# A two-layer hybrid encoder on one core: attention divides its output instead of its probabilities, and VectorE makes all low parts of the mixer's weights

## The chip, the core and the metric

The kernel runs on one core of one Trainium2 chip. The metric is the device time of one launch in microseconds (us). The core has a TensorE for matmuls (PE in the rows; PEld is its weight load), VectorE (DVE), ScalarE (ACT) and GpSimd (POOL) for everything elementwise, and SyncE (SP), which here only issues transfers from device memory. Each engine runs its own queue of instructions in order and waits on semaphores for the others.

## The reference, cut to what matters

Two layers over 512 tokens of width 1024, all in float32. Each layer runs an attention group and a state-space (SSD) group side by side on one normalised input, joins them through one output projection, and then runs a SwiGLU FFN.

```python
def reference(x, ...):
    for i in range(DEPTH):                       # DEPTH = 2
        h = rms_norm(x, norm_mix_w[i])
        proj = jnp.einsum("bld,de->ble", h, w_in[i])
        q, k, v, z, xbc_raw, dt_raw = jnp.split(proj, split_at, axis=-1)
        q = rms_norm(q.reshape(b, l, N_Q_HEADS, HEAD_DIM), q_norm_w[i])    # 8 heads of 64
        k = rms_norm(k.reshape(b, l, N_KV_HEADS, HEAD_DIM), k_norm_w[i])   # 2 heads of 64
        q = axial_rope(q, cos_r, sin_r, cos_c, sin_c)
        k = axial_rope(k, cos_r, sin_r, cos_c, sin_c)
        attn_out = blocked_gqa(q, k, v)
        ssd_out = ssd_mixer(z, xbc_raw, dt_raw, ...)   # conv, chunked scans both ways, gate, norm
        mixed = jnp.concatenate([attn_out, ssd_out], axis=-1)
        x = x + jnp.einsum("ble,ed->bld", mixed, w_out[i])
        h = rms_norm(x, norm_ffn_w[i])
        x = x + swiglu(h, w_gate[i], w_up[i], w_down[i])
    return rms_norm(x, final_norm_w)

def one_block(qi):                               # 128 queries against all 512 keys
    s = jnp.einsum("bqgrd,bkgd->bgrqk", qi, k)
    p = jax.nn.softmax(s, axis=-1)
    return jnp.einsum("bgrqk,bkgd->bqgrd", p, v)
```

## The kernel before

**Products in three parts.** To keep float32 accuracy at the faster matmul type, every weight chunk and every activation is split into a high part (a rounded copy) and a low part (the value minus that copy), and each product is three matmuls: high by high, high by low, low by high. `Stream.split` (lines 180 to 195) makes the parts of a weight chunk of 128x1024: for each 512 columns ScalarE casts `whi` (line 192) and VectorE or GpSimd subtracts to get `wlo` (line 193). Which of the two engines does it is chosen per chunk: the names in `POOL_LO` (line 56) and the four chunks of the SSD half of `w_out` (line 122) go to GpSimd, which makes 16 chunks per layer, 32 in all, in 64 instructions. Chunks are split two ahead of their use.

**The mixer of a layer** (`mixer`, lines 446 to 939) first projects k, v and dt, and then runs three generators by turns (line 930). `fill` goes through `ORDER`: the eight x/B/C chunks with their convolution (`xbc`), the two halves of q (`qproj`) and of z; then, once the SSD half is done, the SSD half of the output projection, `out_half(1, ...)`, 8 output tiles of 12 matmuls; then it waits for attention and splits attention's output into `mixed.h` and `mixed.l` (lines 851 to 855). `ssd` runs the scans and the gated norm and writes its part of `mixed` through `to_mixed`. `att` walks the 8 pairs of a key head g and a block c of 128 queries, four query heads (tiles) each, so 32 tiles per layer. After the three, `out_half(0, ...)` adds the attention half.

**A tile of attention** (lines 663 to 695): two matmuls give the scores in PSUM (668, 669); VectorE takes the negative row maximum (671) and multiplies it by `qri`, the reciprocal norm of the query (672); ScalarE takes the exponential with `qri` as scale and the row sum beside it (674); VectorE takes the sum's reciprocal (675) and multiplies the 128x512 probabilities by it (679); TensorE transposes them in four pieces (682); ScalarE copies them to SBUF (92); TensorE multiplies by the values (692); ScalarE copies the result back into `qr` (92). `queries` prepares the four heads: a ScalarE copy `qd`, four transposes (656), a cast `qh` and a difference `ql` (659, 660).

**Order.** Nothing here is ordered by hand inside an engine. The kernel is traced in the order of the generators, that order gives each instruction its priority, and a planner with a time model of its own lays out each engine's queue when the program is built: the most urgent instruction whose inputs and buffers its model calls ready goes next. On the chip each queue then runs in that fixed order. Helper lines hide several operations: line 92 holds ScalarE copies, line 95 the `tensor_tensor` of VectorE or GpSimd; there one goes by tile names.

The probabilities live in a ring of four 128x512 slots (`ring("p")`), their transposes in another.

Of the kernel before, what the change touches and what calls it, by code (L numbers as in the profile page):

```python
# [15 lines left out]
F32 = mybir.dt.float32  # L16
F32R = mybir.dt.float32r
I32 = mybir.dt.int32
AF = mybir.ActivationFunctionType
# [17 lines left out]
NPAIR = (NF - PLAIN) // 2  # L37
SRAW = 6

NORM = "VVVV"  # L40
PTE = "AAAA"
GGE = "GG"
QDE, OUTE, _, YE, HE, WE, RAE, MLE, DSE = "AAVGVGVVG"
EB, GGB = 2, 4
DDW, DDE = 512, "A"
MORE = "VGGVG"
# [6 lines left out]
YS = 1  # L53
NA, NF_, NS = 1, 2, 3
ORDER = "x4 q0 x5 x7 x6 x3 x0 x1 x2 q1 z0 z1".split()
POOL_LO = "x3 x5 x7 z0 z1 x4 x6 q1 x1".split()
EPS = 1e-6
KVDT = 272

# [11 lines left out]
def merge(a, b, c):  # L71
    return a.rearrange("p (b c) -> p b c", b=b, c=c)


def bc(ap, shape, axis):
    return ap.unsqueeze(axis).broadcast_to(shape)
# [3 lines left out]
def tile_hybrid_encoder(ctx, tc, xt_d, par_d, rope_d, snw_d, w_kvdt, w_xbc, w_q, w_z, w_out, w_gate, w_up, w_down, out_d):  # L80
# [10 lines left out]
    def copy(e, out, in_):  # L91
        A.copy(out, in_) if e == "A" else (G if e == "G" else V).tensor_copy(out, in_)

    def tt(e, *args):
        (G if e == "G" else V).tensor_tensor(*args)
# [9 lines left out]
    def stream(src, n, lo=0, cut=WU):  # L105


        chunks.append((src, n, lo, cut))

    for l in range(L):  # L110
        for i in range(2):
            for j in range(2):
                stream(w_kvdt[l, i, :, 2 * j * KVDT:2 * (j + 1) * KVDT], 2 * KVDT)
        for what in ORDER:
            i, lo = int(what[1]), what in POOL_LO
            if what[0] == "x":
                stream(w_xbc[l, i], 1024, lo, 512)
            else:
                for j in range(2):
                    stream({"q": w_q, "z": w_z}[what[0]][l, 2 * i + j], 1024, lo, 512)  # L120
        for i in range(4):
            stream(w_out[l, 1, i], 1024, 1, 512)
        for i in (2, 3, 0, 1):
            stream(w_out[l, 0, i], 1024, 0, 512)
        for f in range(PLAIN):
            stream(w_gate[l, f], 1024)
            stream(w_up[l, f], 1024)
        for a, b in PHASES:
            for f in range(max(a, PLAIN), b, 2):
                pairs.append((l, f))  # L130
                for what in PRODUCTS:
                    chunks.append((len(pairs) - 1, what, None, WU))
            for m in range(KT):
                stream(w_down[l, m, :, a * P:b * P], (b - a) * P)
# [311 lines left out]
    def mixer(l, norm, mx):  # L446
# [199 lines left out]
        def ring(which):  # L646
            turn[which] += 1
            return rings[which][:, turn[which] % 4]

        def queries(c, g):  # L650

            qd = mx.tile([P, 4, 2, 64], F32, name="qd", tag="qd")
            copy(QDE, qd, bc(qr[:, c, 4 * g:4 * g + 4], [P, 4, 2, 64], 2))
            tp = bank("t")
            for j in range(4):
                T.transpose(tp[:, j * P:(j + 1) * P], qd[:, j].rearrange("p a d -> p (a d)"), ident)
            qh = mx.tile([P, S], F32R, name="qh", tag="qh", bufs=2)
            ql = mx.tile([P, S], F32R, name="ql", tag="ql", bufs=2)
            A.copy(qh, tp)
            V.tensor_tensor(ql, tp, qh.bitcast(F32), ALU.subtract)  # L660
            return qh, ql

        def attention(c, g, qh, ql):
            nm = mx.tile([P, 4], F32, name="nm", tag="nm", bufs=2)
            sm = mx.tile([P, 4], F32, name="sm", tag="sm", bufs=2)
            for j in range(4):
                s_ = bank("s")
                T.matmul(s_, lhsT=qh[:, j * P:(j + 1) * P], rhs=KK[:, g], start=True, stop=False)
                T.matmul(s_, lhsT=ql[:, j * P:(j + 1) * P], rhs=KK[:, g], start=False, stop=True)
                ri = qri[g][:, c, j:j + 1]  # L670
                V.tensor_reduce(nm[:, j:j + 1], s_, AX.X, ALU.max, negate=True)
                V.tensor_tensor(nm[:, j:j + 1], nm[:, j:j + 1], ri, ALU.mult)
                p_ = ring("p")
                A.activation(p_, s_, AF.Exp, bias=nm[:, j:j + 1], scale=ri, accum_out=sm[:, j:j + 1])
                V.reciprocal(sm[:, j:j + 1], sm[:, j:j + 1])
                if NORM[j] == "A":
                    A.activation(p_, p_, AF.Copy, scale=sm[:, j:j + 1])
                else:
                    (G if NORM[j] == "G" else V).tensor_scalar(p_, p_, sm[:, j:j + 1], None, ALU.mult)
                t_ = bank("t")  # L680
                for kt in range(NC):
                    T.transpose(t_[:, kt * P:(kt + 1) * P], p_[:, kt * P:(kt + 1) * P], ident)
                pt = merge(ring("t"), NC, P)
                copy(PTE[j], pt, merge(t_, NC, P))
                if j % 2 == 0:
                    first = pt
                    continue
                o_ = bank(O_BANK)

                for kt in range(NC):  # L690
                    for e, t2 in enumerate((first, pt)):
                        T.matmul(o_[64 * e:64 * e + 64, :P], lhsT=Vt[:, kt, g * 64:(g + 1) * 64],
                                 rhs=t2[:, kt], start=kt == 0, stop=kt == NC - 1)
                copy(OUTE, qr[:, c, 4 * g + j - 1:4 * g + j + 1].rearrange("p h d -> p (h d)"), o_[:, :P])
                yield
# [91 lines left out]
        def out_half(half, order, src, x, nxt=None):  # L787
            for n, m in enumerate(order):
                if n % 2 == 0:
                    wh, wl = W.next()  # L790
                ps = bank("a")
                for k in range(4):
                    o = (n % 2 * 4 + k) * P
                    mm3(ps, wh[:, o:o + P], wl[:, o:o + P], mixed, half * 4 + k, k == 0, k == 3)
                V.tensor_tensor(x[m], src[m], ps, ALU.add)
                if nxt is not None and m >= 4:
                    nxt.tile(m)
                    nxt.square(m)
                if m % 2:
                    yield  # L800
# [21 lines left out]
        def fill():  # L822
            for what in ORDER:
                i = int(what[1])
                if what[0] == "q":
                    yield from qproj(i)
                elif what[0] == "z":
                    yield from token_major(lambda c: bank("a"), op, 256, z_done(i))
                else:
                    xbc(i)  # L830
                    yield
                    if all(f"x{j}" in ORDER[:ORDER.index(what) + 1] for j in range(4, 8)):
                        done.append("BC")
                    if sum(w_[0] == "x" for w_ in ORDER[:ORDER.index(what) + 1]) == 8:
                        for c in range(3):
                            state(0, c)
                        for c in (3, 2, 1):
                            state(1, c)
                        done.append("conv")
            done.append("z")  # L840
            while "ssd" not in done:
                yield

            part = [mx.tile([P, S], F32, name=f"part{i}", tag=t) for i, t in enumerate(sorted(Htags))]
            part += [mx.tile([P, S], F32, name=f"part{6 + i}", tag="ee", bufs=EB) for i in range(2)]
            for k in range(KT):
                nc.sync.dma_start(part[k], (xt_d if l == 0 else x_save)[k])
            yield from out_half(1, range(KT), part, part)
            while "att" not in done:
                yield  # L850
            for j in range(4):
                src = qr.rearrange("p c (j a) d -> p j c (a d)", a=2)[:, j]
                h = mixed.h[j].rearrange("p (c q) -> p c q", c=NC)
                A.copy(h, src)
                tt(MLE, mixed.l[j].rearrange("p (c q) -> p c q", c=NC), src, h.bitcast(F32), ALU.subtract)
            Z["part"] = part

        def drain(*gens):
# [7 lines left out]
        def att():  # L866
            todo = [(c, g) for g in range(2) for c in range(NC)]
            ready = None
            for i, (c, g) in enumerate(todo):
                while g not in qri:  # L870
                    yield
                now = ready or queries(c, g)
                ready = None
                if i + 1 < len(todo) and todo[i + 1][1] in qri:
                    ready = queries(*todo[i + 1])
                yield from attention(c, g, *now)
            done.append("att")

        def finish(cs):
# [288 lines left out]
```

## Time and profile before

| | |
|---|---|
| median of 3 runs | 1262.58 us (1261.21 to 1265.16) |
| the profiled execution | 1260.2 us, of which 1258.5 us are its span |
| mean granted TensorE clock | 0.982 |
| busy: TensorE, VectorE, ScalarE, GpSimd | 96%, 76%, 49%, 20% of the span |
| mixers | about 0 to 290 us and 636 to 900 us |
| FFNs | about 290 to 636 us and 900 to 1250 us |

A page of the profile gives busy time of each engine, the span in slices, and the chain of work that ended last, followed back from the end. Busy shares are averages over the stages, so the views below cut the span into stretches. In rows of windows the columns are the stretch and its length, the busy time of PE, PEld, DVE, ACT and POOL with the count of their instructions, the granted TensorE clock as a share of full speed, the busy share of the DMA engines, and GB/s. In rows of instructions a name such as `wlo<-wraw,whi` says what is written from what.

### The profile page before, as it was taken

How to read it: one execution, taken by the hardware profiler on the slowest of the kernel's cores; microseconds unless marked ns; L12 is line 12 of the kernel's file. 1: busy time of each engine (PE TensorE's matmuls, PEld its weight loads, DVE VectorE, ACT ScalarE, POOL GpSimd, SP SyncE). 2: the span in 40 equal slices, each digit the busy share in tenths (PEclk: the TensorE clock that was granted, in tenths of full speed). 3: DMA queues.
4: the chain of work that ended last, by engine and by line, in shares of the span. 5: the costliest groups of instructions: out<-in, count | busy, mean ns of one | idle time of the engine just before them, and what ended most of it. 6: DMA issues, size and time to landing. Idle time of an engine off the chain costs nothing.

```text
span 1258.5 us, 19786 instructions
## 1 busy us (share of the span) xinstructions
PE 1205.1 (96%) x7694; PEld 1066.4 (85%) x7694; DVE 962.1 (76%) x1593; ACT 620.1 (49%) x1147; POOL 249.3 (20%) x208
## 2 busy tenths in 40 slices
PE   6898998999999999999998999999999999999996
PEld 6787887687899899899897787777878999999995
DVE  8899789656887577577679989985688856856853
ACT  4566655634354244255455575753453533533544
POOL 6523655010200000000234255520120000000002
PEclk8999998999999999999999999989999999999998
DMA  5321122032434324321442202112243233243122
GB/s 170 104 72 51 34 68 77 17 101 65 154 96 143 89 83 132 88 87 32 135 135 89 67 30 72 55 40 72 94 144 88 98 117 113 74 120 114 34 63 80
DMA packets 47533, 110.04 MB, mean 87 GB/s; under 512 B 5424, under 2 KB 5936, under 8 KB 47440
## 3 DMA queue, kind: packets, MB, share of 16 engines
q1 hardware_dynamic: 47440, 108.79, 27.4%
q8 instruction: 60, 0.98, 0.3%
q14 instruction: 33, 0.27, 0.1%
HBM read 104.44 MB, written 4.33 MB: 86 GB/s over the span
## 4 chain that ended last, share of the span: by engine, by line
PE 76%; DVE 17%; ACT 3%; issue 2%; POOL 1%; DMA 1%; DVEq 0%; ACTq 0%; POOLq 0%
PE ps_a L1030 6%; PE ps_a L1029 5%; PE ps_a L1028 5%; PE ps_a L411 4%; PE ps_a L412 3%; PE ps_a L413 3%; PE ps_a L1075 3%; PE ps_a L1074 3%; PE ps_a L1076 3%; PE ps_s L1074 3%; PE ps_s L1075 3%; PE ps_s L1076 3%; PE ps_s L1030 3%; PE ps_s L1029 3%; PE ps_s L1028 3%; DVE u L594 3%
## 5 line engine op out<-in xcount | busy, mean ns | idle before, releaser
L192 ACT CAST whi<-wraw 128x512 fp32r<-128x512 f32 (+4 forms) x185 | 126.7, 713 | 231.7 <-PE ps_a L412 61.5
L192 ACT CAST whi<-sraw 128x1024 fp32r<-128x1024 f32 x126 | 131.7, 1050 | 141.3 <-DVE sraw L167 40.4
L193 DVE TENSOR_TENSOR wlo<-sraw,whi 128x1024 fp32r<-128x1024 f32 x126 | 153.6, 1223 | 46.5 <-ACT whi L192 46.3
L323 POOL TENSOR_TENSOR ssq<-ssq,sqt 128x512 f32<-128x512 f32 x17 | 25.7, 1511 | 679.5 <-ACT sqt L320 679.3
L193 DVE TENSOR_TENSOR wlo<-wraw,whi 128x512 fp32r<-128x512 f32 (+4 forms) x121 | 109.1, 911 | 49.8 <-ACT whi L192 48.8
L411 PE MATMUL ps_a<-xh,whi 128*128 128x512 f32 x320 | 126.3, 397 | 3.2 <-DVE a__9140 L971 1.6
L413 PE MATMUL ps_a<-xh,wlo 128*128 128x512 f32 x320 | 126.0, 394 | 0.0
L412 PE MATMUL ps_a<-xl,whi 128*128 128x512 f32 x320 | 125.7, 394 | 0.0
L193 POOL TENSOR_TENSOR wlo<-wraw,whi 128x512 fp32r<-128x512 f32 x64 | 91.1, 1441 | 97.8 <-ACT whi L192 90.7
L167 DVE TENSOR_TENSOR sraw<-sraw 128x1024 f32<-128x1024 f32 x72 | 88.0, 1222 | 1.0
L419 PE MATMUL ps_a<-whi,xh 128*128 128x256 f32 (+1 forms) x256 | 75.5, 297 | 7.9 <-ACT whi L192 7.8
L1030 PE MATMUL ps_a<-ss,wlo 128*128 128x256 f32 x288 | 81.7, 284 | 0.0
L1028 PE MATMUL ps_a<-ss,whi 128*128 128x256 f32 x288 | 81.5, 283 | 0.0
L1029 PE MATMUL ps_a<-ss,whi 128*128 128x256 f32 x288 | 81.5, 283 | 0.0
L1030 PE MATMUL ps_a<-s,wlo 128*128 128x256 f32 x288 | 81.1, 283 | 0.0
L1029 PE MATMUL ps_a<-s,whi 128*128 128x256 f32 x288 | 81.1, 283 | 0.0
L1028 PE MATMUL ps_a<-s,whi 128*128 128x256 f32 x288 | 79.8, 283 | 0.0
L420 PE MATMUL ps_a<-wlo,xh 128*128 128x256 f32 (+1 forms) x256 | 75.8, 296 | 1.7 <-DVE wlo L193 1.7
L411 PEld LDWEIGHTS ps_a<-xh,whi 128*128 128x128 f32 x320 | 60.2, 188 | 17.1 <-ACT s L989 4.0
L421 PE MATMUL ps_a<-whi,xl 128*128 128x256 f32 (+1 forms) x256 | 74.4, 293 | 0.0
L413 PEld LDWEIGHTS ps_a<-xh,wlo 128*128 128x128 f32 x320 | 60.4, 189 | 13.2 <-issue 0.8
L412 PEld LDWEIGHTS ps_a<-xl,whi 128*128 128x128 f32 x320 | 60.3, 188 | 12.4 <-DVE xl L809 0.4
(393 smaller groups left out, 3601.8 us busy)
## 6 DMA issues: line engine op xcount, KB each, us to landing
sraw<-in_w_gate SPq DMA_DIRECT2D x72, 256.0 KB, 3.8
sraw<-in_w_up SPq DMA_DIRECT2D x72, 256.0 KB, 3.8
wraw<-in_w_down SPq DMA_DIRECT2D x48, 384.0 KB, 3.1
wraw<-in_w_xbc SPq DMA_DIRECT2D x16, 512.0 KB, 3.3
wraw<-in_w_out SPq DMA_DIRECT2D x16, 512.0 KB, 3.3
wraw<-in_w_q SPq DMA_DIRECT2D x8, 512.0 KB, 3.2
wraw<-in_w_z SPq DMA_DIRECT2D x8, 512.0 KB, 3.6
wraw<-in_w_gate SPq DMA_DIRECT2D x8, 512.0 KB, 3.3
```

What stands on the lines that cost most here:

```text
L167: V.tensor_tensor(q[to], q[to], q[by], ALU.add)
L192: A.copy(hi[:, u], raw[:, u])
L193: (G if lo_pool else V).tensor_tensor(lo[:, u], raw[:, u], hi[:, u].bitcast(F32), ALU.subtract)
L411: T.matmul(ps, lhsT=wh, rhs=op.h[k], start=first, stop=False)
L412: T.matmul(ps, lhsT=wh, rhs=op.l[k], start=False, stop=False)
L413: T.matmul(ps, lhsT=wl, rhs=op.h[k], start=False, stop=last)
L420: T.matmul(ps, lhsT=xh, rhs=wl, start=False, stop=False)
L1028: T.matmul(out, lhsT=wh[:, o:o + P], rhs=x_[:, 0, i], start=first and i + j == 0, stop=False, skip_group_check=True)
L1029: T.matmul(out, lhsT=wh[:, o:o + P], rhs=x_[:, 1, i], start=False, stop=False, skip_group_check=True)
L1030: T.matmul(out, lhsT=wl[:, o:o + P], rhs=x_[:, 0, i], start=False, stop=i == 3, skip_group_check=True)
L1074: T.matmul(ps[:, cols], lhsT=w1[:, o:o + P], rhs=h, start=f == a, stop=False)
L1075: T.matmul(ps[:, cols], lhsT=w1[:, o:o + P], rhs=g, start=False, stop=False)
```

## The change

Five things change, all in the mixers.

1. The queries carry their norm: `queries` makes `qd` with four ScalarE activations, one per head, each scaled by `qri`, in place of one copy. The multiplication of the maximum by `qri` (line 672) and the scale in the exponential go.
2. The probabilities stay undivided: the reciprocal (675) and the multiplication of the 128x512 probabilities (679) go. The row sums of all tiles are kept in `sums`.
3. A new function `normalize`, once per layer, when attention and z are done: it takes the reciprocal of all sums, transposes them, spreads them over 128 partitions with four matmuls by a 0/1 matrix `sel`, multiplies attention's output by the result, and makes the parts `mixed.h` and `mixed.l`. It is traced with high priority.
4. `fill` waits for attention ahead of `out_half(1)`, so the SSD half of the output projection is traced after `normalize`; the splitting of attention's output moves from the end of `fill` into `normalize`.
5. `POOL_LO` is empty and the SSD half of `w_out` has its flag at 0: VectorE makes every `wlo` of the mixer.

```diff
-NORM = "VVVV"
-QDE, OUTE, _, YE, HE, WE, RAE, MLE, DSE = "AAVGVGVVG"
+OUTE, _, YE, HE, WE, RAE, MLE, DSE = "AVGVGVVG"
-POOL_LO = "x3 x5 x7 z0 z1 x4 x6 q1 x1".split()
+POOL_LO = ""
...
-            stream(w_out[l, 1, i], 1024, 1, 512)
+            stream(w_out[l, 1, i], 1024, 0, 512)
...
         def queries(c, g):
-            copy(QDE, qd, bc(qr[:, c, 4 * g:4 * g + 4], [P, 4, 2, 64], 2))
+            for j in range(4):
+                A.activation(qd[:, j], bc(qr[:, c, 4 * g + j], [P, 2, 64], 1), AF.Copy, scale=qri[g][:, c, j:j + 1])
...
+        sums = mx.tile([P, NC, 8], F32, name="sums")
+        def normalize():
+            sel = ring("p")[:8]
+            G.memset(sel, 0.0)
+            pick = merge(sel, 8, 64)
+            G.affine_select(out=pick, in_=pick, pattern=[[-1, 8], [0, 64]], compare_op=ALU.not_equal, fill=1.0,
+                            base=0, channel_multiplier=1)
+            rec = mx.tile([P, NC, 8], F32, name="rec")
+            V.reciprocal(rec, sums)
+            tp = bank("t")
+            for c in range(NC):
+                T.transpose(tp[:8, c * P:(c + 1) * P], rec[:, c], ident)
+            rows = ring("p")[:8]
+            A.copy(rows, tp[:8])
+            for j in range(4):
+                b = bank("s")
+                T.matmul(b, lhsT=sel[:, j * P:(j + 1) * P], rhs=rows, start=True, stop=True)
+                o = qr.rearrange("p c (j a) d -> p j c (a d)", a=2)[:, j]
+                V.tensor_tensor(o, o, merge(b, NC, P), ALU.mult)
+                h = merge(mixed.h[j], NC, P)
+                A.copy(h, o)
+                tt(MLE, merge(mixed.l[j], NC, P), o, h.bitcast(F32), ALU.subtract)
...
         def attention(c, g, qh, ql):
                 V.tensor_reduce(nm[:, j:j + 1], s_, AX.X, ALU.max, negate=True)
-                V.tensor_tensor(nm[:, j:j + 1], nm[:, j:j + 1], ri, ALU.mult)
                 p_ = ring("p")
-                A.activation(p_, s_, AF.Exp, bias=nm[:, j:j + 1], scale=ri, accum_out=sm[:, j:j + 1])
-                V.reciprocal(sm[:, j:j + 1], sm[:, j:j + 1])
-                if NORM[j] == "A":
-                    A.activation(p_, p_, AF.Copy, scale=sm[:, j:j + 1])
-                else:
-                    (G if NORM[j] == "G" else V).tensor_scalar(p_, p_, sm[:, j:j + 1], None, ALU.mult)
+                A.activation(p_, s_, AF.Exp, bias=nm[:, j:j + 1], accum_out=sums[:, c, 4 * g + j:4 * g + j + 1])
...
         def fill():
-            yield from out_half(1, range(KT), part, part)
             while "att" not in done:
                 yield
-            for j in range(4):
-                src = qr.rearrange("p c (j a) d -> p j c (a d)", a=2)[:, j]
-                h = mixed.h[j].rearrange("p (c q) -> p c q", c=NC)
-                A.copy(h, src)
-                tt(MLE, mixed.l[j].rearrange("p (c q) -> p c q", c=NC), src, h.bitcast(F32), ALU.subtract)
+            yield from out_half(1, range(KT), part, part)
...
         def att():
+            while "z" not in done:
+                yield
+            with tc.high_priority():
+                normalize()
             done.append("att")
```

## Rows read from the trace of the kernel before

**Rows 1.** The page: the span; the busy time of each engine; the chain that ended last, by engine.

```profile
span 1258.5 us, 19786 instructions
PE 1205.1 (96%) x7694; PEld 1066.4 (85%) x7694; DVE 962.1 (76%) x1593; ACT 620.1 (49%) x1147; POOL 249.3 (20%) x208
PE 76%; DVE 17%; ACT 3%; issue 2%; POOL 1%; DMA 1%; DVEq 0%; ACTq 0%; POOLq 0%
```

**Rows 2.** Windows by stage: the mixer of layer 0 without its start, an FFN, and the mixer of layer 1 in two pieces.

```profile
40.00:290.00 250.00, 234.32 (x1441) 195.38 (x1440) 209.36 (x459) 141.63 (x345) 93.42 (x79) 0.97 0.19 61
310.00:636.00 326.00, 324.41 (x2159) 300.12 (x2158) 240.01 (x262) 146.08 (x186) 15.03 (x9) 1.00 0.35 106
636.00:680.00 44.00, 41.89 (x261) 37.74 (x261) 39.20 (x110) 22.56 (x69) 19.83 (x18) 0.96 0.28 92
680.00:900.00 220.00, 209.59 (x1306) 172.43 (x1305) 183.02 (x379) 126.89 (x296) 78.17 (x65) 0.98 0.19 62
```

**Rows 3.** Windows of 20 us in layer 0's mixer.

```profile
40.00:60.00 20.00, 16.48 (x94) 13.91 (x92) 19.70 (x57) 10.89 (x42) 12.54 (x12) 0.97 0.19 59
100.00:120.00 20.00, 16.55 (x99) 13.76 (x98) 19.73 (x34) 10.65 (x21) 7.75 (x6) 0.93 0.22 76
200.00:220.00 20.00, 15.76 (x92) 12.72 (x92) 18.86 (x37) 8.75 (x21) 10.97 (x9) 0.83 0.32 106
```

**Rows 4.** Waits of PE, in 40 to 250 us (first three rows) and in 640 to 870 us (last two): who waited for whom, us in total, times, the longest.

```profile
PE ps_m L775 <- DVE y L770: 4.2, 1, 4.2
PE ps_m L512 <- DVE acw L509: 3.7, 1, 3.7
PE ps_t L682 <- DVE ql L660: 3.4, 1, 3.4
...
PE ps_m L775 <- DVE y L770: 3.6, 1, 3.6
PE ps_t L682 <- DVE ql L660: 2.4, 1, 2.4
```

**Rows 5.** Windows cut around five of the falls of the granted clock (the column behind POOL's).

```profile
209.00:216.00 7.00, 7.00 (x31) 5.32 (x30) 6.33 (x17) 0.27 (x1) 5.13 (x5) 0.51 0.33 112
820.00:827.00 7.00, 7.00 (x29) 6.37 (x28) 6.96 (x11) 0.59 (x1) 3.99 (x3) 0.51 0.37 112
59.00:66.00 7.00, 5.78 (x24) 5.25 (x25) 6.97 (x27) 4.77 (x9) 2.74 (x3) 0.51 0.22 75
117.00:120.50 3.50, 3.50 (x17) 3.40 (x17) 3.50 (x9) 2.03 (x4) 0.00 (x0) 0.51 0.36 131
731.40:734.80 3.40, 3.40 (x15) 2.75 (x15) 3.40 (x10) 1.60 (x6) 0.00 (x0) 0.50 0.29 112
```

**Rows 6.** Timeline at 202 to 209 us: two rows of VectorE, one of GpSimd (start, length, instruction, count, and in brackets the idle time before it and what ended it).

```profile
203.35 3.44 DVE L95 TENSOR_TENSOR xl<-qr,xh 128x512 fp32r<-128x512 f32 x2
206.72 1.21 DVE L672 TENSOR_TENSOR nm<-nm,qri 128x1 f32<-128x1 f32 x1
...
202.07 5.84 POOL L193 TENSOR_TENSOR wlo<-wraw,whi 128x512 fp32r<-128x512 f32 x4 [4.64 <-ACT whi L192]
```

**Rows 7.** The lines that go, over the whole span: count, duration in ns (least, median, most), first and last start.

```profile
L679 DVE TENSOR_SCALAR p_ring<-p_ring,sm x64: 470/486/1522, 86.6 to 848.0; 128x512 f32<-128x512 f32 x64
L672 DVE TENSOR_TENSOR nm<-nm,qri x64: 140/150/1222, 84.2 to 846.2; 128x1 f32<-128x1 f32 x64
L675 DVE RECIPROCAL sm<-sm x64: 136/155/165, 85.8 to 847.8; 128x1 f32<-128x1 f32 x64
```

**Rows 8.** Groups of instructions: the low part of a 128x512 weight piece on VectorE and on GpSimd, and the splitting of attention's output on VectorE (count, busy us, mean ns, idle before).

```profile
L193 DVE TENSOR_TENSOR wlo<-wraw,whi 128x512 fp32r<-128x512 f32 x48 | 32.9, 707 | 7.0 <-ACT whi L192 7.0
L193 POOL TENSOR_TENSOR wlo<-wraw,whi 128x512 fp32r<-128x512 f32 x64 | 91.1, 1441 | 97.8 <-ACT whi L192 90.7 <-PE ps_m L524 7.0
L95 DVE TENSOR_TENSOR xl<-qr,xh 128x512 fp32r<-128x512 f32 x8 | 8.6, 1091 | 0.2
```

**Rows 9.** The same line 193 and line 679 in the front of the mixers, 40 to 120 us (first two rows) and 660 to 740 us (last two).

```profile
L193 POOL TENSOR_TENSOR wlo<-wraw,whi x16: 1253/1392/1842, 44.3 to 114.4; 128x512 fp32r<-128x512 f32 x16
L679 DVE TENSOR_SCALAR p_ring<-p_ring,sm x6: 474/486/1517, 86.6 to 104.6; 128x512 f32<-128x512 f32 x6
...
L193 POOL TENSOR_TENSOR wlo<-wraw,whi x15: 1271/1343/1749, 659.5 to 728.4; 128x512 fp32r<-128x512 f32 x15
L679 DVE TENSOR_SCALAR p_ring<-p_ring,sm x8: 479/484/1522, 700.6 to 737.6; 128x512 f32<-128x512 f32 x8
```

**Rows 10.** Prices for what is new: ScalarE's copies of 128x512 and of 128x128 (groups; both are line 92), and from the chain of waits a matmul of 512 columns in plain float32 (two instructions) and eight transposes (start, length, what).

```profile
L92 ACT COPY qd<-qr 128x512 f32<-128x512 f32 x16 | 10.1, 631 | 3.6 <-DVE qr L95 3.5
L92 ACT COPY qr<-ps_t 128x128 f32<-128x128 f32 x32 | 8.5, 267 | 13.9 <-PE ps_t L692 13.4
...
913.65 0.86 PE ps_m L344 x2
...
840.43 1.02 PE ps_t L682 x8
```

**Rows 11.** The end of the mixers: the matmuls of line 411 (one of the three of each product of `out_half`; 32 in an `out_half`) in 236 to 250 and 842 to 866 us, PE and PEld columns only; and the values' matmuls with their first and last start.

```profile
236.00:250.00 14.00, 6.37 (x17) 3.00 (x17) 1.00 0.12 39
842.00:866.00 24.00, 9.69 (x25) 4.57 (x25) 1.00 0.14 44
...
L692 PE MATMUL ps_t<-t_ring,Vt x512: 272/273/477, 95.4 to 865.7; 128*64 128x128 f32 x171
```

More of the change, by code (lines that the diff above doesn't have):

```diff
@@ L661, in queries @@
             return qh, ql
+        sums = mx.tile([P, NC, 8], F32, name="sums")
[20 more added lines that the diff above has]
+                tt(MLE, merge(mixed.l[j], NC, P), o, h.bitcast(F32), ALU.subtract)
         def attention(c, g, qh, ql):
             nm = mx.tile([P, 4], F32, name="nm", tag="nm", bufs=2)
-            sm = mx.tile([P, 4], F32, name="sm", tag="sm", bufs=2)
             for j in range(4):
@@ L669, in attention @@
                 T.matmul(s_, lhsT=ql[:, j * P:(j + 1) * P], rhs=KK[:, g], start=False, stop=True)
-                ri = qri[g][:, c, j:j + 1]
                 V.tensor_reduce(nm[:, j:j + 1], s_, AX.X, ALU.max, negate=True)
-                V.tensor_tensor(nm[:, j:j + 1], nm[:, j:j + 1], ri, ALU.mult)
                 p_ = ring("p")
-                A.activation(p_, s_, AF.Exp, bias=nm[:, j:j + 1], scale=ri, accum_out=sm[:, j:j + 1])
-                V.reciprocal(sm[:, j:j + 1], sm[:, j:j + 1])
-                if NORM[j] == "A":
-                    A.activation(p_, p_, AF.Copy, scale=sm[:, j:j + 1])
-                else:
-                    (G if NORM[j] == "G" else V).tensor_scalar(p_, p_, sm[:, j:j + 1], None, ALU.mult)
+                A.activation(p_, s_, AF.Exp, bias=nm[:, j:j + 1], accum_out=sums[:, c, 4 * g + j:4 * g + j + 1])
                 t_ = bank("t")
```

## The prediction, made before the change was run

> **What bounds the kernel now.** I read the page first: TensorE is busy 96% of the span and carries 76% of the chain that ended last, VectorE 17% [rows 1]. Then the windows by stage: the FFNs leave TensorE nothing (324.41 of 326 us), so whatever moves must move in the mixers. There TensorE is idle for 250 - 234.32 = 15.7 us in layer 0 and 2.1 + 10.4 us in layer 1, 28.2 us in all. The granted clock there is 0.97, 0.96 and 0.98: with two levels, full and half, the time lost is (1 - share) times the stretch, 7.5 + 1.8 + 4.4 = 13.7 us [rows 2]. So 41.9 us is the ceiling of what any relief of the other engines gives.
>
> The windows of 20 us say which engine holds TensorE up: in 40 to 60 and 100 to 120 us VectorE is busy 19.7 of 20 us while TensorE is idle 3.5 [rows 3]. The list of TensorE's waits agrees: its five longest, 17.3 us together, all end on a VectorE instruction [rows 4]. Behind these idle times the clock stands at the 1.2 GHz level (0.50 to 0.51) for 7.0, 7.0, 7.0, 3.5 and 3.4 us [rows 5], half of which is lost, 14.0 us. The waits with their falls: the two at line 775 cost 4.2 + 3.6 + 7.0 = 14.8 us, the two for `ql` 3.4 + 2.4 + 3.5 = 9.3, the one at line 512 3.7 + 3.5 = 7.2; together 31.3 of the 41.9.
>
> One more thing is to be seen: why VectorE is late. At 203.35 us, while GpSimd makes four `wlo`, two `xl` take 3.44 us and a one-column multiplication 1.21 us [rows 6], where its median is 0.150 [rows 7] and a subtraction of the same size takes 0.707 [rows 8]. A VectorE instruction that meets a GpSimd one loses up to that one's whole length.
>
> **VectorE's account.** Removed: 64 tiles lose lines 679, 672 and 675, at medians 0.486 + 0.150 + 0.155 = 0.791 us each [rows 7], 50.6 us. Added: 64 `wlo` pieces at 0.707 us [rows 8], 45.2 us; in `normalize` 8 multiplications of 128x512, which I price like that subtraction, 5.7 us, and two small reciprocals, 0.3 us. The 8 subtractions to `mixed.l` only move. By these counts VectorE gains nothing: +0.6 us.
>
> The gain is in what GpSimd no longer holds up. The trace has no VectorE without those 64 GpSimd instructions, so I bound it. From below 0: the moved pieces may be held up by GpSimd's other work as much as others were by them. From above: in rows 6 the three instructions lost (3.44 - 1.41) + (1.21 - 0.15) = 3.1 us beside four `wlo`, 0.77 us each, so 64 x 0.77 = 49 us. I take two thirds, 33 us, nearer to the upper end because the medians of rows 7 against their maxima (486 and 1522, 150 and 1222 ns) show the loss to be the ordinary length of one GpSimd instruction.
>
> The change puts a wait into VectorE's queue: each moved `wlo` waits for ScalarE's `whi`, and behind it stand the conv, the maxima and the scan steps that TensorE waits for. VectorE's own 48 waited 7.0 us in all, 0.15 each; GpSimd's 64 waited 90.7 us, but GpSimd had little else to do [rows 8]. The bounds are 64 x 0.15 = 9.3 us and 90.7; I take the lower, VectorE's own. Net VectorE relief: 33 - 9.3 - 0.6, some 23 us.
>
> By the Trainium skill, page "Perfetto Trace Analysis", section "Optimizing Scalar/DVE Operations", a saturated VectorE is a reason to hand work to ScalarE or even GpSimd, though it warns that GpSimd and VectorE share a read port. Taken alone the first half says that this change goes the wrong way; that is the rival S below. The rows side with the warning, as far as the one stretch of rows 6 goes.
>
> **TensorE's account.** New on the engine that is 96% busy: 8 matmuls with `sel`, 512 columns in plain float32, like line 344 at 0.86 us, and 8 small transposes at 1.02/8 = 0.13 us [rows 10]: 6.9 + 1.0 = 7.9 us. Nothing is removed there. This is paid in full, since TensorE has work ahead and behind it.
>
> **ScalarE and GpSimd.** `qd` goes from 16 x 0.631 = 10.1 us to 64 x 0.267 = 17.1 us, +7.0, and two copies of `rows` come, at most 1.3 us [rows 10]. ScalarE is 49% busy [rows 1], so I put these at nothing; uncovered they would cost at most 8.3 us. The new wait of `qd` for `qri` I put at nothing too: line 672, which goes, waited for the same value two steps later. GpSimd keeps a memset and a select per layer. SyncE's transfers keep their order: the `part` loads already stood ahead of this wait, and the loads of `w_out` follow the chunk order, which is unchanged.
>
> **Stall by stall.** The two waits at line 775 I take as gone, 14.8 us: what VectorE did then, the two `xl` beside four GpSimd `wlo` [rows 6], is no longer there, since `xl` now comes after all of attention. Of the `ql` and line-512 waits, 16.5 us, I take half: VectorE's queue ahead of them is relieved but still full. In the fronts, 40 to 120 and 660 to 740 us, 31 pieces come (21.9 us with 0.707 each) and 14 tiles lose 0.791 us (11.1 us) [rows 9], +10.8 us, against a freed 2/3 x 31 x 0.77 = 16: relief there is only 5 us. Of the other 41.9 - 31.3 = 10.6 us I take half, 5.3. Sum: 14.8 + 8.2 + 5.3 = 28.3 us won, 7.9 paid, 20.4 us less.
>
> **The end of the mixer.** `normalize` is a chain: 0.16 (reciprocal), 0.5 (transposes), 0.63 (copy), 0.86 (matmul), 0.71 (multiplication), 0.63 (cast), 0.71 (subtraction), 4.2 us to the first quarter, and 1.4 us of VectorE for each of the next three, 8.4 us. Its cover is what is left of `out_half(1)`. In the windows that end where attention ends, 250 us and 866 us (the last values' matmul starts at 865.7), 17 and 25 of its 32 products were made [rows 11], so 15 and 7 are left; a product took at most 14.0/17 = 0.82 us, attention beside it, and I take 0.7: 10.5 and 4.9 us. Layer 0 is covered; in layer 1 up to 3.5 us may show, less what `out_half(0)` can start on the first quarter. I count 0 and keep 3.5 for the range.
>
> **The rivals.** *B, VectorE no longer bounds at all*: the freed 49 us in full, and each stall and fall goes: 41.9 - 7.9 = 34.0 us less, 1228.6. For it speaks that all long waits end on VectorE [rows 4]; against it that the fronts stay near full.
>
> *T, the cover is gone*: `out_half(1)`, traced later, is used up as filler before attention ends, or the planner's model puts TensorE's `sel` matmuls into its queue earlier than the chip has their input. Then 8.4 us per layer lie open, each with a fall of the clock like the shortest ones, half of 7.0: 2 x (8.4 + 3.5) = 23.8 us on top, +3.4 against before, 1266. It decides from the point where less than 4 us of `out_half(1)` is left; layer 1 is near it.
>
> *S, a saturated VectorE takes work on* (slower): the port's waits pass to the moved pieces and nothing is freed. Then the fronts get +10.8 us and 31 waits for `whi` of 0.15 us, 4.6; TensorE pays 7.9; only the 14.8 us of line 775 are won: +8.5 us, 1271. It decides if a moved `wlo` takes over 1.2 us instead of 0.7: 64 x 0.5 = 32 us is all that I count as freed. That the change does nothing can't be: `POOL_LO` has 64 GpSimd instructions to show [rows 8].
>
> **How the numbers follow.** The profiled execution took 1260.2 us, 2.4 under the median of 1262.6, so I add 2.4: forecast 1260.2 - 20.4 + 2.4 = 1242. Chances: forecast 0.57, B 0.17, T 0.12, S 0.14. B is 1260.2 - 34.0 + 2.4 = 1228.6. The range reaches down to 1218, which is B and 10 us more for matmuls that run slowly inside TensorE's busy time, which these rows don't count, and up to 1268, which takes in T and the lower part of S with the 3.5 us of the mixer's end; some 0.2 is left out. A measurement of this kernel can tell 0.3%, 3.8 us, from no change. Faster by more: forecast, B and a quarter of T, 0.77; within: 0.09; slower: S, 0.14.
>
> **What would show it.** In the profile after: no GpSimd `wlo`; VectorE's `wlo` of 128x512 near 0.7 us (S: over 1.2); VectorE's busy time some 30 to 60 us below 962.1; the waits at line 775 gone and with them the falls near 209 and 820 us; TensorE's idle time in the mixers near half of 28.2 us. Wrong it would be if TensorE waits for `wlo` in the fronts (S), or for VectorE in `normalize` at the mixers' ends (T), or if the planner's new order has long waits in places where there are none now.

## The result, and the profile after

The changed kernel takes 1233.32 us (median of 4 runs, 1231.61 to 1236.18) against 1261.89 for the kernel before: a ratio of 0.9773, with a 95% interval of 0.9754 to 0.9792, 28.6 us less. The forecast was 1242, in a range of 1218 to 1268. The profiled execution of the changed kernel was the slowest of its four, 1236.18 us, so from profile to profile the difference is 24.0 us, where 20.4 were worked out.

The page of the changed kernel: span, busy time of each engine, the chain by engine, to be read against [rows 1].

```profile
span 1234.4 us, 19748 instructions
PE 1204.1 (98%) x7718; PEld 1062.9 (86%) x7718; DVE 911.0 (74%) x1475; ACT 626.9 (51%) x1197; POOL 169.9 (14%) x148
PE 83%; DVE 10%; ACT 2%; issue 2%; POOL 1%; DMA 0%; DVEq 0%; POOLq 0%; ACTq 0%
```

VectorE does 51.1 us less, though by the prediction's counts it was given 0.6 us more than was taken from it. Its share of the chain falls from 17 to 10%.

Windows of the changed kernel: the three mixer stretches of [rows 2], and three of the stretches of [rows 5].

```profile
40.00:290.00 250.00, 245.71 (x1510) 202.79 (x1509) 191.90 (x409) 146.41 (x363) 57.27 (x53) 0.99 0.21 66
636.00:680.00 44.00, 44.00 (x232) 37.03 (x231) 41.34 (x124) 28.15 (x78) 9.00 (x8) 1.00 0.25 82
680.00:900.00 220.00, 216.01 (x1333) 175.97 (x1332) 160.07 (x308) 129.69 (x313) 52.95 (x46) 0.98 0.19 59
...
209.00:216.00 7.00, 7.00 (x45) 5.57 (x44) 3.11 (x5) 3.60 (x10) 1.17 (x2) 1.00 0.01 2
59.00:66.00 7.00, 7.00 (x32) 5.56 (x31) 7.00 (x21) 4.14 (x7) 0.90 (x2) 1.00 0.18 66
117.00:120.50 3.50, 3.50 (x28) 3.33 (x27) 2.76 (x4) 3.50 (x14) 3.23 (x3) 1.00 0.00 0
```

TensorE's idle time in the mixers was 15.7 + 2.1 + 10.4 = 28.2 us and is 4.3 + 0.0 + 4.0 = 8.3 us. What the clock costs there, (1 - share) times the stretch, was 13.7 us and is 2.5 + 0.0 + 4.4 = 6.9. Together 19.9 + 6.8 = 26.7 us won. The three old falls that are shown here are gone (1.00 where 0.51 stood). The list of TensorE's waits over the whole span agrees: those that end on VectorE came to 28.9 us before and come to 6.2 us now, and none ends on GpSimd in either kernel.

The longest waits of TensorE in the changed kernel, in 40 to 250 us (first three rows) and 640 to 870 us (the rest); line 793 is what was line 775 in [rows 4].

```profile
PE ps_m L793 <- DVE y L788: 1.4, 1, 1.4
PE ps_t L710 <- ACT t_ring L91: 1.0, 1, 1.0
PE ps_t L700 <- ACT qr L91: 0.8, 1, 0.8
...
PE ps_t L700 <- ACT t_ring L91: 0.8, 1, 0.8
PE ps_m L793 <- DVE y L788: 0.5, 1, 0.5
```

The two waits at the scan's matmul are 1.4 and 0.5 us (4.2 and 3.6 before); those on `ql` and `acw` are in the list no more.

The group of all low parts of 128x512 on VectorE (count, busy us, mean ns, idle before), against [rows 8].

```profile
L192 DVE TENSOR_TENSOR wlo<-wraw,whi 128x512 fp32r<-128x512 f32 x112 | 77.2, 707 | 13.7 <-ACT whi L191 13.5
```

112 pieces in place of 48, the same 707 ns each, and 13.7 us of waiting for `whi` in all, 0.12 each.

But the clock falls at two new places. Windows cut around them, layer 0 and layer 1, and the timeline of TensorE just ahead of the first (start, length, what):

```profile
242.50:249.30 6.80, 6.80 (x16) 4.49 (x15) 3.21 (x6) 1.24 (x2) 0.00 (x0) 0.50 0.24 78
839.90:850.10 10.20, 10.20 (x19) 5.51 (x19) 5.08 (x9) 2.50 (x5) 0.00 (x0) 0.50 0.16 51
```

```profile
237.51 1.98 PE L682 MATMUL ps_s<-p_ring 8*128 8x512 f32 x4
239.42 0.50 PE L412 MATMUL ps_a<-xh,wlo 128*128 128x512 f32 x1
...
240.55 1.12 PE L682 MATMUL ps_s<-p_ring 8*128 8x512 f32 x2
241.60 0.51 PE L410 MATMUL ps_a<-xh,whi 128*128 128x512 f32 x1
242.03 1.59 PE L682 MATMUL ps_s<-p_ring 8*128 8x512 f32 x2
243.55 0.80 PE L411 MATMUL ps_a<-xl,whi 128*128 128x512 f32 x1
```

TensorE is not idle there (6.80 of 6.80 and 10.20 of 10.20 us), yet its clock stands at the 1.2 GHz level. Ahead of the fall stand the new `sel` matmuls of `normalize`, which use 8 of the 128 rows (the `8x512` of their moving operand). Half of 17.0 us, 8.5 us, is lost.

### The profile page after: what moved, and what is told of

The parts are those of the page before. It is cut to its first block, busy times and chain, and to the rows that moved or that the text cites. A ratio compares the mean times of both kernels' runs of the same rounds, so it can differ in the third digit from the quotient of the medians.

```text
span 1234.4 us, 19748 instructions
## 1 busy us (share of the span) xinstructions
PE 1204.1 (98%) x7718; PEld 1062.9 (86%) x7718; DVE 911.0 (74%) x1475; ACT 626.9 (51%) x1197; POOL 169.9 (14%) x148
## 3 DMA queue, kind: packets, MB, share of 16 engines
HBM read 104.44 MB, written 4.33 MB: 88 GB/s over the span
## 4 chain that ended last, share of the span: by engine, by line
PE 83%; DVE 10%; ACT 2%; issue 2%; POOL 1%; DMA 0%; DVEq 0%; POOLq 0%; ACTq 0%
PE ps_a L1047 6%; PE ps_a L1046 6%; PE ps_a L1045 6%; PE ps_a L410 5%; PE ps_a L411 5%; PE ps_a L412 5%; PE ps_a L1092 3%; PE ps_a L1091 3%; PE ps_a L1093 3%; PE ps_s L1091 3%; PE ps_s L1092 3%; PE ps_s L1093 3%; PE ps_s L1047 3%; PE ps_s L1046 3%; PE ps_s L1045 3%; PE ps_t L710 3%
## 5 line engine op out<-in xcount | busy, mean ns | idle before, releaser
L192 DVE TENSOR_TENSOR wlo<-wraw,whi 128x512 fp32r<-128x512 f32 (+4 forms) x185 | 153.3, 840 | 56.5 <-ACT whi L191 55.3
L410 PEld LDWEIGHTS ps_a<-xh,whi 128*128 128x128 f32 x320 | 61.6, 193 | 23.1 <-ACT s L1006 4.0
L412 PEld LDWEIGHTS ps_a<-xh,wlo 128*128 128x128 f32 x320 | 61.4, 192 | 14.7 <-issue 2.0
L1091 PE MATMUL ps_s<-hid,whi 128*128 128x512 f32 (+1 forms) x182 | 69.9, 384 | 0.0
```

The lines of the kernel that those rows point to most:

```text
L192: (G if lo_pool else V).tensor_tensor(lo[:, u], raw[:, u], hi[:, u].bitcast(F32), ALU.subtract)
L410: T.matmul(ps, lhsT=wh, rhs=op.h[k], start=first, stop=False)
L412: T.matmul(ps, lhsT=wl, rhs=op.h[k], start=False, stop=last)
L1091: T.matmul(ps[:, cols], lhsT=w1[:, o:o + P], rhs=h, start=f == a, stop=False)
```

## The experiments

Three theories stood against each other. **P**: GpSimd's 64 subtractions held VectorE's instructions up, and taking them away is what helps. **A**: the leaner tile of attention and the later `xl` are what helps. **Q** (after the first runs): VectorE is not held; GpSimd's queue, with its waits for `whi`, gave its own results late.

**Each half alone.** `attn_only` is the changed kernel with GpSimd's low parts back; `wlo_only` is the kernel before with all low parts on VectorE. The same two lines, either way:

```diff
-POOL_LO = ""
+POOL_LO = "x3 x5 x7 z0 z1 x4 x6 q1 x1".split()
-            stream(w_out[l, 1, i], 1024, 0, 512)
+            stream(w_out[l, 1, i], 1024, 1, 512)
```

> The change without its weights part: GpSimd makes the 64 low parts again (POOL_LO as before, flag 1 for the SSD half of w_out), attention divides its output. Theory P (most of the gain comes from GpSimd no longer holding VectorE up): the 50 us of VectorE's attention work go, the 49 us of holding up stay, VectorE's busy time falls to about 915 to 925 us, and the time comes to 1246 to 1256 us. Theory A (the shorter attention is the gain, and where the low parts are made hardly matters): within 5 us of the whole change, 1230 to 1238 us.

> The weights part alone: the kernel before with all low parts on VectorE. Theory P: 45 us of subtractions come to VectorE, about 49 us of holding up go, its busy time stays within 10 us of 962, TensorE's waits behind GpSimd's subtractions go, 1252 to 1262 us. Theory A and rival S (a saturated VectorE takes work on): VectorE over 990 us, new waits of TensorE, 1266 to 1278 us.

`attn_only` took 1269.71 us (9 runs, 1265.69 to 1273.32), ratio 1.0054 [1.0037, 1.0072]: slower than before, outside the ranges of both theories, though VectorE's busy time is where P had it (921.9 us, 915 to 925 expected). `wlo_only` took 1236.91 us (4 runs), ratio 0.9802 [0.9779, 0.9826], better than P's range. So the weights' half alone gives nearly all, and the attention half alone costs. Their busy times:

```profile
PE 1216.0 (96%) x7718; PEld 1070.1 (84%) x7718; DVE 921.9 (73%) x1411; ACT 626.8 (49%) x1197; POOL 250.0 (20%) x212
```

is `attn_only`, and `wlo_only` is

```profile
PE 1192.7 (97%) x7694; PEld 1057.0 (86%) x7694; DVE 953.4 (77%) x1657; ACT 622.8 (50%) x1147; POOL 167.7 (14%) x144
```

The half that takes 40.2 us off VectorE's busy time (962.1 to 921.9) is slower by 7 us; the half that takes off 8.7 us is faster by 25. Here the busy time of an engine with slack does not price a change. What was held up does: the counted work and the measured differ by 962.1 + 45.2 - 953.4 = 53.9 us in `wlo_only`, by 962.1 + 0.6 - 911.0 = 51.7 in the full change, and by 962.1 - 50.6 + 6.0 - 921.9 = -4.4, nothing freed, in `attn_only`.

Where it shows is the wait at line 793. VectorE's timeline in `attn_only`, then GpSimd's and TensorE's of the same kernel:

```profile
196.85 0.16 DVE L289 TENSOR_TENSOR yri0t<-yri0t,ym 128x4 f32<-128x4 f32 x1
...
197.44 1.14 DVE L289 TENSOR_TENSOR yri0t<-yri0t,ym 128x4 f32<-128x4 f32 x1
198.61 1.20 DVE L290 SCALAR_TENSOR_TENSOR yri<-yri0t,yri 128x4 f32<-128x4 f32 x1
199.84 4.67 DVE L912 SCALAR_TENSOR_TENSOR xs<-xs,yri,snw 128x256 f32<-128x256 f32 x4
```

```profile
197.28 5.15 POOL L192 TENSOR_TENSOR wlo<-wraw,whi 128x512 fp32r<-128x512 f32 x4 [3.44 <-ACT whi L191]
202.39 1.44 POOL L94 TENSOR_TENSOR gg<-gg,ee 128x512 f32<-128x512 f32 x1
```

```profile
205.50 0.79 PE L793 MATMUL ps_m<-H,CT 128*128 128x256 f32 x1 [4.33 <-DVE y L788]
```

`xl` is gone from here, as in the full change, and TensorE still waits 4.33 us (4.2 before): now it is instructions of 128x4 that take 1.14 and 1.20 us (0.16 for the first of them at 196.85 us) and `xs`, 4.67 us for four (2.69 in the changed kernel); GpSimd's subtractions beside them take 5.15 / 4 = 1.29 us each. In `wlo_only` the two `xl` are still in their old place, and no subtraction of GpSimd beside them:

```profile
190.00 0.69 DVE L95 TENSOR_TENSOR xl<-qr,xh 128x512 fp32r<-128x512 f32 x1
...
190.75 0.68 DVE L95 TENSOR_TENSOR xl<-qr,xh 128x512 fp32r<-128x512 f32 x1
```

They take 0.69 and 0.68 us in place of 3.44 for two [rows 6], and the wait at line 775, as it is numbered there, is 1.1 us:

```profile
PE ps_m L775 <- DVE y L770: 1.1, 1, 1.1
```

This refutes A, and with it the reason that the prediction gave for the end of these waits.

**The order of `out_half(1)`.** `order_back` traces it ahead of attention's wait again:

```diff
+            yield from out_half(1, range(KT), part, part)
             while "att" not in done:
                 yield
-            yield from out_half(1, range(KT), part, part)
```

> The whole change, but the SSD half of the output projection is traced ahead of the wait for attention, as before, so that the normalizing chain comes last. If the order is what hides the chain of 8.4 us per layer: TensorE idle behind the SSD half, 8 to 20 us slower than the change, 1241 to 1253 us. If the planner lays out the same queues either way: within 3 us of 1233.

1233.24 us, ratio 0.9774 [0.9739, 0.9809]: the same as the full change. The trace order of that half decides nothing here; `normalize`, traced with high priority, comes among the products of `out_half(1)` in both.

**The rows of `sel`.** `rows128` lets the `sel` matmuls run over 128 rows, the other 120 of `sel` being zero:

```diff
-            sel = ring("p")[:8]
+            sel = ring("p")
-            rows = ring("p")[:8]
-            A.copy(rows, tp[:8])
+            rows = ring("p")
+            A.copy(rows[:8], tp[:8])
```

> The whole change with one edit: the matmuls that spread the reciprocals read all 128 rows of their two operands (120 of them zero in sel) instead of 8. If the two falls of the clock at the mixers' ends (6.8 and 10.2 us at half) come from matmuls that use 8 of 128 rows: both falls go and 5 to 8 us are won, 1225 to 1229 us. If they come from anything else there: same falls, within 3 us of 1233.

1227.99 us, ratio 0.9726 [0.9704, 0.9749], 5.3 us under the changed kernel and in the expected range. The instructions stand in the same order on TensorE, VectorE, ScalarE and SyncE. Its windows at the first place of the fall and in the mixer of layer 1:

```profile
242.50:249.30 6.80, 6.80 (x28) 4.72 (x26) 5.11 (x10) 2.35 (x5) 0.00 (x0) 1.00 0.22 78
...
826.00:850.00 24.00, 23.67 (x107) 17.33 (x106) 14.74 (x23) 9.98 (x17) 1.41 (x2) 1.00 0.21 72
```

The granted clock is 1.00 in both, and this kernel has no fall behind 40 us until its end: the falls behind `normalize` came with the 8-row matmuls. By its medians the attention half is now worth 1236.9 - 1228.0 = 8.9 us on top of the weights' half, against 3.6 with 8 rows.

**Giving GpSimd its work back, without use.** Four kernels leave the changed kernel's computation as it is and add spare work to GpSimd whose result nobody reads, at the 64 pieces that it made before: the same subtraction into a spare tile (`spare_sub`); a subtraction of two constant masks that waits for no `whi` (`spare_const`); two memsets, which read nothing (`spare_set`); and one column of the subtraction, with all its waits and a third of its length (`spare_touch`; 0.47 us each, where some 0.1 had been expected). One line `spare = ...` for each; `old` holds the chunks that `POOL_LO` and the flag of `w_out` gave GpSimd before.

```diff
+    spare = lambda r, h, s: G.tensor_tensor(s, r, h.bitcast(F32), ALU.subtract)   # spare_sub
+    spare = lambda r, h, s: G.tensor_tensor(merge(s, 4, P), bc(mask["le"], [P, 4, P], 1), bc(mask["ge"], [P, 4, P], 1), ALU.subtract)   # spare_const
+    spare = lambda r, h, s: [G.memset(s, v) for v in (0.0, 1.0)]   # spare_set
+    spare = lambda r, h, s: G.tensor_tensor(s[:, :1], r[:, :1], h[:, :1].bitcast(F32), ALU.subtract)   # spare_touch
...
-                    (G if lo_pool else V).tensor_tensor(lo[:, u], raw[:, u], hi[:, u].bitcast(F32), ALU.subtract)
+                    (G if lo_pool else V).tensor_tensor(lo[:, u], raw[:, u], hi[:, u].bitcast(F32), ALU.subtract); spare(raw[:, u], hi[:, u], nrm.tile([P, S], F32, name="spare", tag="sqt", bufs=2)) if j in old else None
```

> The whole change, and beside each of the 64 moved subtractions GpSimd makes the same subtraction into a spare tile that nobody reads, so GpSimd reads, waits for ScalarE's high part and holds the port as in the kernel before, while VectorE's results are the ones used. Theory P (the port): VectorE's busy time goes up by 40 to 55 us over 911, and 12 to 25 us of time come back: 1245 to 1258 us. Theory Q (what slowed the kernel before were GpSimd's results, late because GpSimd is slow or because its other work stood behind these waits): the results are no longer GpSimd's, but its other work stands behind the waits again, so 3 to 12 us come back, without a rise of VectorE's busy time over 925.

> As the run with spare subtractions, but the 64 spare ones read two constant masks, so they wait for nothing; they still read two tiles and write one of 128x512. Theory P: as there, VectorE's busy time up by 30 to 55 us, 10 to 25 us come back, 1243 to 1258 us. Theory Q: no waits in GpSimd's queue, so within 4 us of 1233.

> As before, but the spare work is two memsets of 128x512 for each moved subtraction, about 1.06 us of GpSimd that writes and reads nothing. Theory P in its plain form (whoever comes second waits, whatever GpSimd does): 8 to 20 us come back. Theory P with reads only (a VectorE instruction with two inputs meets GpSimd's reads, not its writes): within 4 us of 1233, VectorE's busy time within 10 us of 911. Theory Q: within 4 us of 1233.

> As the run with spare subtractions, waits included, but each spare subtraction takes one column, about 0.1 us of GpSimd. Theory P: nothing to hold up, within 4 us of 1233. Theory Q: GpSimd's other work stands behind the same waits, 3 to 12 us come back, 1236 to 1245 us.

| | us (4 runs each) | ratio to before | VectorE busy in the profile |
|---|---|---|---|
| changed kernel | 1233.32 | 0.9773 [0.9754, 0.9792] | 911.0 |
| `spare_touch` | 1236.92 | 0.9789 [0.9773, 0.9804] | 911.6 |
| `spare_set` | 1251.53 | 0.9900 [0.9874, 0.9927] | 923.6 |
| `spare_const` | 1283.15 | 1.0151 [1.0135, 1.0167] | 972.4 |
| `spare_sub` | 1285.78 | 1.0185 [1.0144, 1.0226] | 972.9 |

The groups of the spare instructions, of `spare_touch`, `spare_const` and `spare_sub` in turn (count, busy us, mean ns, idle before and what ended it):

```profile
L101 POOL TENSOR_TENSOR spare<-wraw,whi 128x1 f32<-128x1 f32 x64 | 29.3, 470 | 124.8 <-ACT whi L191 86.7 <-issue 35.7 <-DVE ssq L322 1.1
```

```profile
L101 POOL TENSOR_TENSOR spare<-m_le,m_ge 128x512 f32<-128x512 f32 x64 | 95.0, 1507 | 23.5 <-PE ps_m L343 19.4 <-DVE ssq L322 3.2
```

```profile
L101 POOL TENSOR_TENSOR spare<-wraw,whi 128x512 f32<-128x512 f32 x64 | 97.4, 1541 | 103.5 <-ACT whi L191 61.5 <-issue 40.7 <-DVE ssq L322 1.1
```

All the waits of the old subtractions, with a third of their length, cost 3.6 us by the medians, and the intervals overlap; this lies in the ranges of both P and Q. Their length without the waits costs 49.8, where Q expected no more than 4: the waits for `whi` are not what slowed the kernel before. That GpSimd gave its own results late because it was busy longer is another form of Q, and the lists of waits speak against it. In `spare_const` TensorE's waits that end on VectorE rise from 6.2 to 36.8 us over the span, those that end on GpSimd from 0 to 2.0, and VectorE's own waits for GpSimd from 3.7 to 4.2 (3.3 in the kernel before); only in `spare_sub` are 5.0 us of TensorE's waits GpSimd's.

In `spare_const` and `spare_sub` VectorE runs the same 1475 instructions as in the changed kernel, in another order, and is busy 61.4 and 61.9 us longer, 0.96 and 0.97 us for each spare instruction of 1.5 us. Both also come out above P's ranges, in time and in VectorE's busy time: each spare instruction holds up more than an old one did (0.81 to 0.84 us each, by the 51.7 and 53.9 above). Why it does was not tested; the planner lays them elsewhere.

One kind of VectorE instruction that is not held up can be read from `spare_const`: the row maxima, which read PSUM, kept their length with 64 subtractions about (at most 693 ns in the changed kernel too). Line 695 there (count, ns least, median, most, first and last start):

```profile
L695 DVE TENSOR_REDUCE nm<-ps_s x64: 673/683/693, 120.8 to 858.0; 128x1 f32<-128x512 f32 x64
```

The Trainium skill, page "SBUF — State Buffer", section "Who interferes with whom", says that VectorE and GpSimd share one pair of SBUF ports, that the one that issues first keeps the other out for its whole instruction, that a reduction on trn2 never contends, and that a VectorE instruction with two SBUF inputs contends with GpSimd's reads and not with its writes alone. The trace agrees on the reductions (at most 693 ns) and on the two-input steps (1.14 us in place of 0.16). On writes alone `spare_set` bears it out for the subtractions (least 676 and median 693 ns on line 192, 675 and 692 in the changed kernel; the longest, 5882 ns, stood behind the copies shown next). But `spare_set` took 18.2 us more than the changed kernel, where the expectation for reads alone was within 4, and it shows another case: copies. Its VectorE at 65 us, with the same copies of layer 1, and then its GpSimd at 65 us:

```profile
65.75 0.41 DVE L94 TENSOR_TENSOR qr<-t,t 128x256 f32<-128x256 f32 x1
66.08 6.31 DVE L508 COPY acw<-ac 128x32 f32<-128x32 f32 x4
...
66.51 5.88 DVE L192 TENSOR_TENSOR wlo<-wraw,whi 128x512 fp32r<-128x512 f32 x1
...
671.22 8.74 DVE L508 COPY acw<-ac 128x32 f32<-128x32 f32 x4
```

```profile
65.21 7.66 POOL L101 MEMSET spare<- 128x512 f32 x16
```

Four copies of 128x32, 0.24 us each on average in the changed kernel, take 6.31 us beside 16 memsets in a row, and the subtraction behind them ends when they do, at 72.39 us. The same page says that copies may, under conditions, use both ports and then contend with any GpSimd instruction. The trace agrees in that the copies were held up; whether they meet the conditions no run shows. They waited not for one memset but for nearly the whole row of them. Much of the 18.2 us lies at two such rows of memsets, since TensorE's cumulative sums at line 511 take `acw`: its waits in 40 to 90 and in 650 to 700 us, 12.6 us together, are the two below. The second is put down to a spare memset, which TensorE does not read; the matmul starts at 680.13 us, behind the end of the copies at 671.22 + 8.74 = 679.96.

```profile
PE ps_m L511 <- DVE u L593: 4.9, 1, 4.9
...
PE ps_m L511 <- POOL spare L101: 7.7, 1, 7.7
```

**Is the attention half bad without the falls?** `attn_128` is `attn_only` with the four lines of `rows128`.

> The change without its weights part (GpSimd makes the 64 low parts), with the matmuls that spread the reciprocals on all 128 rows. Alone, the attention part came to 1269.7 us, 7 us slower than before, with VectorE's busy time 40 us lower. If what it pays is TensorE's 7.9 us and falls of the clock behind the 8-row matmuls (3.4 + 10.2 + 6.8 us at half in that run): some 5 to 8 us less, 1261 to 1265 us, about the kernel before. If it is slower because VectorE is held up at worse moments: within 3 us of 1269.7.

1262.08 us (10 runs), ratio 0.9997 [0.998, 1.0014], as expected: the 8-row matmuls made `attn_only` slower than before, and with 128 rows 40 us less of VectorE's time buys nothing. Of the three falls that the expectation counts, the one of 10.2 us was not theirs: it began at 817.7 us, by the wait at line 793, and the two behind the 8-row matmuls cost half of 3.4 + 6.8, 5.1 us. TensorE's waits in 40 to 250 us (first three rows) and 640 to 870 us say why the time off VectorE bought nothing:

```profile
PE ps_m L793 <- DVE y L788: 4.3, 1, 4.3
PE ps_m L511 <- DVE acw L508: 3.6, 1, 3.6
PE ps_m L764 <- DVE st L750: 2.3, 1, 2.3
...
PE ps_m L793 <- DVE y L788: 3.6, 1, 3.6
```

The waits at lines 775 and 512 of [rows 4] are here at their old length. The two for `ql` (3.4 + 2.4 us) are gone; against them stand a new one of 2.3 us and TensorE's added matmuls.

**More of the same.** `ropes_v` and `all_v` start from `rows128` and move further work of GpSimd to VectorE: one more part of the rotary step, or all that the mixer's letters allow.

```diff
-MORE = "VGGVG"
+MORE = "VGGVV"      # ropes_v
+MORE = "VVVVV"      # all_v, with the next two
+GGE = "VV"
+OUTE, _, YE, HE, WE, RAE, MLE, DSE = "AVVVVVVV"
```

> The 128-row version of the change (1228.0 us), and the second product of the rotary embedding moves from GpSimd to VectorE as well (24 instructions per two layers in each of two sizes: about 0.41 us for 128x256 and 0.28 us for 128x128 there, against 1.02 and 0.85 us on GpSimd). Theory P: 16 x 0.41 + 8 x 0.28 = 9 us come to VectorE, up to 23 us of holding up go, the fronts gain: 2 to 8 us faster, 1220 to 1226 us. Rival S (a saturated VectorE takes work on): 2 to 6 us slower, 1230 to 1234 us.

> The 128-row version of the change with every elementwise product of the mixers on VectorE (rotary products, the masks' and the skip's products, the sums of the scans, the gate). About 55 us of work come to VectorE, and GpSimd keeps only the masks' set-up, the sums of squares and one product of each FFN tile. Theory P without a limit: VectorE's busy time rises by less than 15 us and the time falls to 1215 to 1226 us. If the limit is VectorE's own work, which is over 90% in the mixers: 1228 to 1240 us.

`ropes_v`: 1226.21 us, ratio 0.9716 [0.9698, 0.9733]. `all_v`: 1225.82 us, ratio 0.9718 [0.9698, 0.9739], with VectorE busy 926.2 us (910.5 in `rows128`) and GpSimd 64.7. Neither can be told from `rows128` (0.9726); the first lies just outside P's range of 1220 to 1226, the second just inside its 1215 to 1226, with 15.7 us more of VectorE where less than 15 was expected. What GpSimd still holds up there seems to stand ahead of no wait of TensorE. All three beat both kernels.

## Why the prediction was right, point by point

**The bound, right.** The gain came from TensorE's waits on VectorE in the mixers and the falls behind them: 26.7 of the ceiling of 41.9 us. TensorE's waits that end on VectorE went from 28.9 to 6.2 us.

**What VectorE was freed of: the right mechanism, sized too low.** The step "I take two thirds, 33 us" measured 51.7 us, just above its upper end of 49; 0.81 us for each moved piece, where the one stretch of rows 6 had given 0.77. That stretch was the rule and not the bad case. Not every VectorE instruction is held up, though: the row maxima were not.

**The wait for `whi`, right.** 13.7 us for 112 pieces against 9.3 + 7.0 worked out.

**The two waits at line 775, right size, wrong cause.** The step that failed is that what VectorE did then "is no longer there, since `xl` now comes after all of attention". `attn_only` moves `xl` and keeps the wait (4.33 us); `wlo_only` keeps `xl` and loses it. In `attn_only` steps of the norm and `xs` meet GpSimd's four subtractions there in place of `xl`, and they are held up as it was. The waits shrank to 1.4 and 0.5 us because the subtractions went.

**The other waits, too low.** "I take half" of the `ql` and line-512 waits and of the rest: those at line 512 and for `ql` went altogether, and idle time fell by 19.9 us, not by half of 28.2. The "only 5 us" of relief in the fronts were probably too low for the same reason as the 33 us; no run measures the fronts by themselves.

**TensorE's new work, too low.** The price of 7.9 us left out the two falls behind the 8-row matmuls, 8.5 us of the clock; `rows128` gets 5.3 of them back. Without this, the time was rival B's: `rows128` took 1228.0 where B gave 1228.6. That B's number was met is in part luck, since 8.3 us of idle time are left in the changed kernel's mixers that B took as gone. And that the forecast came as near as 9 us is luck in part too: the relief was put too low and the falls were left out, and the two errors offset each other.

**ScalarE and the mixers' end, put at nothing: right.** ScalarE does 6.8 us more (626.9 against 620.1), and TensorE's waits that end on it went only from 12.5 to 14.5 us over the span. No idle time of TensorE shows in the two windows behind `normalize`.

**The sum.** 26.7 won by the windows less 7.9 paid is 18.8; profile to profile it is 24.0. Of the 5.2 us between them 3.2 are idle time outside these windows: over the whole span TensorE's idle time fell from 1258.5 - 1205.1 = 53.4 us to 1234.4 - 1204.1 = 30.3, by 23.1. The other 2.0 us are within the rounding of the clock shares to 0.01, some 2.6 us either way in each kernel. The median fell by 28.6 because the changed kernel's profiled execution was the slowest of its four and that of the kernel before, 1260.26 us, the fastest.

**The rivals.** T did not come: TensorE is not idle in the windows behind `normalize`, and `order_back` shows that the trace order is not what covers it. S is refuted by the 707 ns. The Trainium skill's first half, which spoke for S (page "Perfetto Trace Analysis", section "Optimizing Scalar/DVE Operations"), is outweighed here by its warning on the shared port: the 25 us of `wlo_only` are work taken back from GpSimd.

**Open.** Each of these edits, the two halves of the change too, also makes the planner lay out other queues. By the traces, the longest sequence of VectorE instructions that keeps its order has 1283 of 1593 between the kernel before and `wlo_only`, and 1285 of 1475 between the changed kernel and `spare_const`. So how much of the 25 us of `wlo_only` and of the 50 us of `spare_const` is order and how much is holding up was not separated; VectorE's 61.4 us at the same 1475 instructions is what is measured. Order alone is a weak rival: `ropes_v` and `all_v` reorder the queue of `rows128` as much (1305 and 1246 of 1475 in the same order) and come within 2.2 us of it. And what in an 8-row matmul lowers the clock was not tried beyond 8 against 128 rows.

## What to carry to other kernels

Price an engine's work by what its instructions hold up on others: compare a VectorE row's median with its longest, look at what GpSimd runs beside the long ones, and take a two-input GpSimd subtraction of 1.5 us as up to 1 us of VectorE's time, even when its result is never waited for. Ask of busy time taken off an engine whether it stood right ahead of a wait of the engine that bounds: 40 us off VectorE gave 0 in `attn_128`, 9 us off gave 25 in `wlo_only`. When a small matmul is added amid dense ones, look at the granted clock behind it, and try it over all 128 rows.

## What the runs showed of the hardware that was not expected

The TensorE clock stood at the 1.2 GHz level for 6.8 and 10.2 us while TensorE was never idle, behind 8 matmul instructions over 8 rows; with the same queues and 128 rows it stayed at the 2.4 GHz level. And a VectorE copy of 128x32 that met 16 GpSimd memsets in a row got through only after 6 us, longer than any single instruction of GpSimd there.
